# Gate and up of both SwiGLUs by seven block products, their result through DRAM, and down as a stage of its own

## The chip, the cores and the metric

One Trainium2 chip, one of its cores. The metric is the device time of one launch in microseconds, the median of several runs. The engines have the names of the profile: PE (TensorE, with its weight loads as PEld), DVE (VectorE), ACT (ScalarE), POOL (GpSimd), SP (SyncE, which only issues transfers here).

## The reference

One layer of a decoder for 1088 tokens (1024 of a prompt, 8 × 8 of samples), width 1024, inner width 2816. The parts that the change touches are the two SwiGLUs:

```python
def rmsnorm(x, g):
    xf = x.astype(jnp.float32)
    xf = xf * lax.rsqrt(jnp.mean(xf * xf, axis=-1, keepdims=True) + NORM_EPS)
    return (xf * g.astype(jnp.float32)).astype(x.dtype)

def swiglu(x, w_gu, w_down):
    gate, up = jnp.split(x @ w_gu, 2, axis=-1)
    return (jax.nn.silu(gate) * up) @ w_down
...
    h = x + 0.5 * swiglu(rmsnorm(x, lp['norm_ffn1']), lp['ffn1_gu'], lp['ffn1_down'])
    n = rmsnorm(h, lp['norm_mix'])
    proj = n @ lp['w_in']
...
    h = h + jnp.concatenate([o_g, o_s], axis=-1) @ lp['w_out']
    h = h + 0.5 * swiglu(rmsnorm(h, lp['norm_ffn2']), lp['ffn2_gu'], lp['ffn2_down'])
    h = h + jax.nn.sigmoid(rmsnorm(h, lp['norm_ple']) @ lp['ple_gate']) * (p @ lp['ple_proj'])
```

Between `proj` and `h + ...` lies the mixing phase: a gated delta rule and a windowed attention. The last line before the output is the per-layer embedding, followed by a final norm.

## The kernel before

Rows (features) lie on the 128 partitions in eight blocks `k` (KD = 8), tokens on the columns. The 1088 tokens are cut into three column chunks `CH` of 416, 416 and 256. Every fp32 factor of a product is split exactly into two parts (`split`: ScalarE copies the high part, VectorE subtracts to get the low one), and each product is three matmuls: high by high, high by low, low by high (`acc3`). All matmuls are issued from line 172, all splits are lines 198 (ScalarE) and 199 (VectorE).

Inner width 2816 is 22 blocks `f` of 128. For each f, `gu(f)` loads a gate unit and an up unit (512 KB each, tile `raw`), splits them, and computes for each chunk `pg` and `pu`, 24 matmuls each (8 k × 3): 144 per f. The rows that they multiply are `xh`, `xl`, the parts of h·g; the factor 1/rms (`rB`) is multiplied in afterwards, in `finish`, on `pg` and `pu`. So at f = 0 products can begin before 1/rms is known (`nm.split` first, `nm.sums` behind the products). `finish` leaves the result of f in SBUF (`ah`, `al`, three buffers).

After each pair of f, `down` multiplies the pair by its two units of the down weights: 8 row blocks × 3 chunks × 6 matmuls = 144, and VectorE adds each result, halved, to the rows `h` in SBUF (line 362). The rows h stay in SBUF from the input to the mixing norm.

`last` of the first SwiGLU is `mix_norm` (norm of the mixing phase: split and sums, chunk after chunk; rows are saved to DRAM, `scrH`), of the second `embed` (per-layer embedding and final norm). The sums go: squares (ScalarE, added by GpSimd and VectorE), `pss` (TensorE, sums over partitions), ten small VectorE steps for 1/sqrt (`nrt`, `nry`), a diagonal matrix `dg` (VectorE and GpSimd), `pb` (TensorE, broadcast). After the first SwiGLU come 48 small `pm` matmuls for the decay logits, then the projection by `w_in`. At the end of the mixing phase `out_row` and `out_proj` read back the saved rows and add the output projection (tile `pf`), row block after row block.

All loads of weights and inputs are issued by SP, in one order; results to DRAM by ACT. A tile of a pool with n buffers is loaded or written again only when the instructions that read its n-th last content are done.

## Time and profile before

| what | value |
|---|---|
| time, runs shown | 2394.14, 2399.76, 2397.82 us |
| median | 2397.82 us |
| the profiled execution, its span | 2390.8 us (no other time of this execution is given) |
| median less span | 7.0 us |
| TensorE, VectorE, ScalarE, GpSimd busy | 2328.3, 1275.0, 655.0, 255.8 us |
| granted TensorE clock, mean | 0.984 |
| first SwiGLU, mixing phase, second SwiGLU, embedding | about 0 to 810, 810 to 1443, 1443 to 2237, 2237 to 2391 us |

The span goes from the first to the last instruction; the time of a run has some microseconds around it. Busy times of engines overlap, so they do not add up to the span.

### The profile page before, as it was taken

How to read it: one execution, taken by the hardware profiler on the slowest of the kernel's cores; microseconds unless marked ns; L12 is line 12 of the kernel's file. 1: busy time of each engine (PE TensorE's matmuls, PEld its weight loads, DVE VectorE, ACT ScalarE, POOL GpSimd, SP SyncE). 2: the span in 40 equal slices, each digit the busy share in tenths (PEclk: the TensorE clock that was granted, in tenths of full speed). 3: DMA queues.
4: the chain of work that ended last, by engine and by line, in shares of the span. 5: the costliest groups of instructions: out<-in, count | busy, mean ns of one | idle time of the engine just before them, and what ended most of it. 6: DMA issues, size and time to landing. Idle time of an engine off the chain costs nothing.

```text
span 2390.8 us, 34804 instructions
## 1 busy us (share of the span) xinstructions
PE 2328.3 (97%) x14216; PEld 2262.3 (95%) x14216; DVE 1275.0 (53%) x2582; ACT 655.0 (27%) x1345; POOL 255.8 (11%) x242
## 2 busy tenths in 40 slices
PE   7999999999999999989999999999999999999996
PEld 7999999999999898979987899999999999999896
DVE  8544444444444767875654546444444444444847
ACT  6112111112111455321345534111111111211523
POOL 2000000000000234242320120000000000000324
PEclk9999999999999999999997999999999999999998
DMA  4111111111111235455543622111111111111113
GB/s 165 41 49 48 41 50 39 43 47 50 39 51 30 95 113 157 121 148 185 168 155 118 187 70 73 51 36 54 39 51 41 49 36 54 41 49 40 51 44 119
DMA packets 121549, 181.51 MB, mean 76 GB/s; under 512 B 28623, under 2 KB 86735, under 8 KB 121391
## 3 DMA queue, kind: packets, MB, share of 16 engines
q1 hardware_dynamic: 82640, 145.99, 19.2%
q10 hardware_dynamic: 38751, 33.32, 4.5%
q8 instruction: 111, 1.82, 0.3%
q14 instruction: 47, 0.39, 0.1%
HBM read 140.71 MB, written 37.87 MB: 75 GB/s over the span
## 4 chain that ended last, share of the span: by engine, by line
PE 84%; DVE 8%; DMA 3%; ACT 3%; issue 2%; POOL 0%; ACTq 0%; SPq 0%; DVEq 0%; POOLq 0%
PE pg L172 25%; PE pu L172 21%; PE pd L172 21%; PE pm L172 5%; PE pf L172 3%; DVE cv L512 1%; PE pr L172 1%; PE po L172 1%; DVE solve L653 1%; DVE xl L249 1%; PE plv L172 1%; PE pq L172 1%; DVE solve L654 1%; PE px L951 1%; ACT xh L248 1%
## 5 line engine op out<-in xcount | busy, mean ns | idle before, releaser
L172 PE MATMUL pg<-xh,thi 128*128 128x416 f32 (+1 forms) x1248 | 411.4, 330 | 9.0 <-ACT xh L248 6.0
L172 PE MATMUL pg<-xh,tlo 128*128 128x416 f32 (+1 forms) x1248 | 412.2, 330 | 1.3 <-DVE tlo L199 1.3
L172 PE MATMUL pg<-xl,thi 128*128 128x416 f32 (+1 forms) x1248 | 410.5, 329 | 0.6 <-DVE xl L249 0.6
L362 DVE SCALAR_TENSOR_TENSOR h<-pd,h 128x416 f32<-128x416 f32 (+1 forms) x528 | 279.9, 534 | 187.4 <-PE pd L172 184.9
L172 PE MATMUL pd<-ah,dhi 128*128 128x416 f32 (+1 forms) x1056 | 347.5, 329 | 1.8 <-DVE h L362 1.7
L172 PE MATMUL pu<-xh,ulo 128*128 128x416 f32 (+1 forms) x1056 | 347.4, 329 | 1.0 <-DVE ulo L199 1.0
L172 PE MATMUL pu<-xh,uhi 128*128 128x416 f32 (+1 forms) x1056 | 347.4, 329 | 0.7 <-ACT uhi L198 0.7
L172 PE MATMUL pd<-ah,dlo 128*128 128x416 f32 (+1 forms) x1056 | 346.8, 328 | 0.0
L172 PE MATMUL pd<-al,dhi 128*128 128x416 f32 (+1 forms) x1056 | 346.8, 328 | 0.0
L172 PE MATMUL pu<-xl,uhi 128*128 128x416 f32 (+1 forms) x1056 | 344.7, 326 | 0.0
L338 DVE TENSOR_TENSOR tu<-pu,rB 128x416 f32<-128x416 f32 x132 | 70.7, 536 | 352.2 <-PE pu L172 352.2
L172 PEld LDWEIGHTS pg<-xh,thi 128*128 128x128 f32 x1248 | 236.8, 190 | 11.3 <-ACT xh L248 6.3
L172 PEld LDWEIGHTS pg<-xl,thi 128*128 128x128 f32 x1248 | 236.7, 190 | 3.3 <-DVE xl L249 1.0
L172 PEld LDWEIGHTS pg<-xh,tlo 128*128 128x128 f32 x1248 | 236.7, 190 | 2.9 <-DVE tlo L199 1.5
L172 PEld LDWEIGHTS pd<-ah,dhi 128*128 128x128 f32 x1056 | 199.5, 189 | 5.0 <-DVE h L362 3.3
L172 PEld LDWEIGHTS pd<-al,dhi 128*128 128x128 f32 x1056 | 199.6, 189 | 1.5
L172 PEld LDWEIGHTS pd<-ah,dlo 128*128 128x128 f32 x1056 | 199.6, 189 | 1.4
L172 PEld LDWEIGHTS pu<-xh,ulo 128*128 128x128 f32 x1056 | 198.0, 187 | 3.0 <-DVE ulo L199 1.3
L172 PEld LDWEIGHTS pu<-xh,uhi 128*128 128x128 f32 x1056 | 198.8, 188 | 1.6 <-ACT uhi L198 1.1
L172 PEld LDWEIGHTS pu<-xl,uhi 128*128 128x128 f32 x1056 | 198.9, 188 | 1.3
L172 PE MATMUL pm<-xh,thi 128*128 128x416 f32 (+1 forms) x528 | 179.2, 339 | 11.2 <-DVE pre L498 6.4
L172 PE MATMUL pm<-xl,thi 128*128 128x416 f32 (+1 forms) x528 | 178.8, 339 | 0.0
(302 smaller groups left out, 3338.1 us busy)
## 6 DMA issues: line engine op xcount, KB each, us to landing
raw<-in_gu SPq DMA_DIRECT2D x88, 512.0 KB
raw<-in_dn SPq DMA_DIRECT2D x44, 512.0 KB
raw<-in_w_in SPq DMA_DIRECT2D x22, 512.0 KB
raw<-in_gate SPq DMA_DIRECT2D x16, 512.0 KB
raw<-in_w_out SPq DMA_DIRECT2D x14, 512.0 KB
scrT<-cv ACTq DMA_DIRECT2D x8, 544.0 KB
scrK<-tok ACTq DMA_DIRECT2D x8, 512.0 KB
kv<-scrK SPq DMA_DIRECT2D x8, 512.0 KB
```

The source lines that it names most:

```text
L172: i = T.matmul(out, lhsT=lhsT, rhs=rhs, start=start, stop=stop)
L248: S.activation(out=self.h[ci][k], in_=src, func=AF.Copy, scale=g)
L249: V.scalar_tensor_tensor(out=self.l[ci][k], in0=src, scalar=g, in1=self.h[ci][k].bitcast(F32), op0=ALU.mult, op1=ALU.subtract)
L338: V.tensor_tensor(out=tu, in0=pu, in1=nm.r[ci], op=ALU.mult)
L362: V.scalar_tensor_tensor(out=h[m][:, s], in0=pd, scalar=0.5, in1=h[m][:, s], op0=ALU.mult, op1=ALU.add)
L512: V.scalar_tensor_tensor(out=dst, in0=src, scalar=wj, in1=dst, op0=ALU.mult, op1=ALU.add)
L653: V.tensor_tensor(out=tmp[:, :i, :i], in0=X0[:, :i, :i], in1=bc(F[:, :i, i], 1, i), op=ALU.mult)
L654: V.tensor_reduce(out=X0[:, :i, i], in_=tmp[:, :i, :i], axis=AX.X, op=ALU.add, negate=True)
L951: T.transpose(px[:, kv, kb], sc[:, q, kv, kb * P : (kb + 1) * P], ident)
```

## The change

Both SwiGLUs are cut in two parts. `gate_up` takes the tokens in two halves of 544 (`c`), each of two quarters of 272 (QW). For each f and half, gate and up (two row blocks) of two input halves by two token quarters form a 2 × 2 product of blocks, which is computed by seven block products (`WOPS` by `OPS`, 4 k × 3 = 12 matmuls of 272 columns each) instead of eight. `weights(f)` forms and splits the seven weight operands: A11, A12, A22 are the units' halves, S1 to S4 sums that GpSimd makes in place. `operands(c)` loads the rows of a half (`hq`, in the pool `wh`), makes 1/rms, multiplies the rows by g and 1/rms, and forms and splits the seven row operands: B11, B21, B22, and T1 to T4. `hidden` sums the seven products into gate and up, applies Silu and writes the result to DRAM (`scrU`). f = 0 is done for half 0, then the operands of half 1 are made, then f = 0 for half 1; from f = 1 on both halves alternate.

`ffn` then runs down as a stage of its own: rows h are loaded (x, or `scrO` in the second SwiGLU), and for each chunk of CH all 22 f are summed in eight PSUM banks `pd`; the results are read back from `scrU` (`ar`) and split, and the down weights are loaded and split once per chunk, so three times. The norms that follow split and square chunk after chunk, and make the sums of all three chunks after the last. The output projection (`out_half`) works on halves of 544 and leaves its rows in DRAM (`scrO`). `wr` has four buffers instead of two.

```diff
+QW = NT // 4
+HW = NT // 2
+KH = KD // 2
...
-    wr = ctx.enter_context(tc.tile_pool(name="wr", bufs=2))
-    wh = ctx.enter_context(tc.tile_pool(name="wh", bufs=2))
+    wr = pool(ctx, "wr", 4)
+    wh = pool(ctx, "wh", 2)
+    hs = pool(ctx, "hs", 3)
...
+    def unit(src, eng=V):
+        raw = raw_unit(src)
+        w = wh.tile([P, 2, 1024], F32R, tag="t", name="t")
+        split(w[:, 0], w[:, 1], raw, eng)
+        return w[:, 0], w[:, 1]
...
-    def ffn(w_gu, w_dn, gcol, tag, last, first=None):
...
+    scrU = dr.tile([NF, P, NT], F32, name="scrU")
+    OPS = ("B11", "B21", "T2", "T3", "T4", "T1", "B22")
+    WOPS = ("A11", "A12", "S2", "S3", "A22", "S1", "S4")
+    def gate_up(w_gu, gcol, tag, src):
+            xp = [pool(st, tag + "x0", 1, "right"), None]
+            wp = pool(st, tag + "w", 1, "right")
+            tp = pool(st, tag + "t", 2, "right")
+            ps = pool(st, tag + "ps", 8, space=PSUM)
+            xp[1] = pool(st, tag + "x1", 1)
+            X = []
+            def operands(c):
+                def tile_(o, q):
+                    return xp[c].tile([P, KH, QW], F32R, tag=q + o, name=q + o)
+                x = {o: (tile_(o, "h"), tile_(o, "l")) for o in OPS}
+                q = []
+                for i in range(2):
+                    t0 = (2 * c + i) * QW
+                    hq = wh.tile([P, KD, QW], F32, tag="t", name="hq")
+                    for k, n in ((0, 2), (2, 2), (4, 4)) if not X else ((0, 4), (4, 4)):
+                        nc.sync.dma_start(out=hq[:, k : k + n], in_=src[:, k : k + n, t0 : t0 + QW])
+                    acc = tp.tile([P, CW], F32, tag="sum", name="sum", bufs=1)[:, :QW]
+                    squares(tp, [hq[:, k] for k in range(KD)], acc, QW)
+                    r = rms(ps, "m", tp, QW, acc)
+                    for k in range(KD):
+                        V.scalar_tensor_tensor(out=hq[:, k], in0=hq[:, k], scalar=vecs[:, gcol + k : gcol + k + 1], in1=r,
+                                               op0=ALU.mult, op1=ALU.mult)
+                    q.append(hq)
+                    for o, j in (("B11", 0), ("B21", 1)) if i == 0 else (("B22", 1),):
+                        split(*x[o], hq[:, j * KH : (j + 1) * KH])
+                b11, b21, b12, b22 = (q[i][:, j * KH : (j + 1) * KH] for i in range(2) for j in range(2))
+                for o, out, p_, m_, eng in (("T1", b11, b12, b11, V), ("T3", b12, b22, b12, G), ("T2", b22, b22, b11, V), ("T4", b21, b21, b22, V)):
+                    eng.tensor_tensor(out=out, in0=p_, in1=m_, op=ALU.subtract)
+                    split(*x[o], out)
+                return x
+            def weights(f):
+                g, u = (raw_unit(w_gu[f + NF * i]) for i in range(2))
+                (a11, a12), (a21, a22) = ((x[:, :512], x[:, 512:]) for x in (g, u))
+                w = {o: tuple(wp.tile([P, 512], F32R, tag=q + o, name=q + o) for q in ("h", "l")) for o in WOPS}
+                split(*w["A11"], a11)
+                split(*w["A12"], a12)
+                split(*w["A22"], a22)
+                G.tensor_tensor(out=a22, in0=a22, in1=a21, op=ALU.add)
+                G.tensor_tensor(out=a21, in0=a11, in1=a21, op=ALU.subtract)
+                G.tensor_tensor(out=a11, in0=a22, in1=a11, op=ALU.subtract)
+                split(*w["S2"], a11)
+                split(*w["S3"], a21)
+                split(*w["S1"], a22)
+                G.tensor_tensor(out=a12, in0=a12, in1=a11, op=ALU.subtract)
+                split(*w["S4"], a12)
+                return w
+            def hidden(f, w, cs2):
+                I = {}
+                for c in cs2:
+                    I[c] = {n: tp.tile([P, QW], F32, tag=n, name=n) for n in ("p1", "u2", "u3", "s0", "s1")}
+                    I[c]["act"] = hs.tile([P, HW], F32, tag="row", name="act")
+                    I[c]["o0"], I[c]["o1"] = I[c]["act"][:, :QW], I[c]["act"][:, QW:]
+                def product(i, *then):
+                    for c in cs2:
+                        pt_ = ps.tile([P, 512], F32, tag="m", name="p" + WOPS[i])[:, :QW]
+                        (wh_, wl), (xh, xl) = w[WOPS[i]], X[c][OPS[i]]
+                        acc3(pt_, [(wh_[:, j * P : (j + 1) * P], wl[:, j * P : (j + 1) * P], xh[:, j], xl[:, j]) for j in range(KH)])
+                        for out, x in then:
+                            if x is None:
+                                S.copy(I[c][out], pt_)
+                            else:
+                                V.tensor_tensor(out=I[c][out], in0=I[c][x], in1=pt_, op=ALU.add)
+                product(0, ("p1", None))
+                product(1, ("s0", "p1"))
+                for c in cs2:
+                    S.activation(out=I[c]["s0"], in_=I[c]["s0"], func=AF.Silu)
+                product(2, ("u2", "p1"))
+                product(3, ("u3", "u2"))
+                product(4, ("o0", "u3"))
+                for c in cs2:
+                    G.tensor_tensor(out=I[c]["o0"], in0=I[c]["s0"], in1=I[c]["o0"], op=ALU.mult)
+                product(5, ("u3", "u3"), ("u2", "u2"))
+                product(6, ("s1", "u2"))
+                for c in cs2:
+                    S.activation(out=I[c]["s1"], in_=I[c]["s1"], func=AF.Silu)
+                    V.tensor_tensor(out=I[c]["o1"], in0=I[c]["s1"], in1=I[c]["u3"], op=ALU.mult)
+                    nc.scalar.dma_start(out=scrU[f, :, c * HW : (c + 1) * HW], in_=I[c]["act"])
+            w0 = weights(0)
+            X.append(operands(0))
+            hidden(0, w0, (0,))
+            X.append(operands(1))
+            hidden(0, w0, (1,))
+            for f in range(1, NF):
+                hidden(f, weights(f), (0, 1))
+    def ffn(w_gu, w_dn, gcol, tag, src, last):
+        gate_up(w_gu, gcol, tag, src)
+        st = ExitStack()
+        xg = pool(st, tag + "xg", 1)
+        fr = ExitStack()
+        h1 = pool(fr, tag + "h", 1, "right").tile([P, KD, NT], F32, name="h")
+        fp = pool(fr, tag + "f", 2, "right")
+        ps = pool(fr, tag + "pd", 8, space=PSUM)
+        h = [h1[:, k] for k in range(KD)]
+        for ci, (c0, w) in enumerate(CH):
+            nc.sync.dma_start(out=h1[:, :, c0 : c0 + w], in_=src[:, :, c0 : c0 + w])
+        end = last(xg, ps, fp, h1, h)
+        next(end)
+        for ci, (c0, w) in enumerate(CH):
+            pd = [ps.tile([P, 512], F32, tag="m", name="pd")[:, :w] for m in range(KD)]
+            for f in range(NF):
+                wf = blocks(unit(w_dn[f]))
+                a = fp.tile([P, CW], F32, tag="ar", name="ar", bufs=3)[:, :w]
+                nc.sync.dma_start(out=a, in_=scrU[f, :, c0 : c0 + w])
+                ah, al = (fp.tile([P, CW], F32R, tag=t, name=t)[:, :w] for t in ("ah", "al"))
+                split(ah, al, a)
+                for m in range(KD):
+                    mm(pd[m], wf[m][0], ah, start=f == 0, stop=False)
+                    mm(pd[m], wf[m][0], al, start=False, stop=False)
+                    mm(pd[m], wf[m][1], ah, start=False, stop=f == NF - 1)
+            for m in range(KD):
+                V.scalar_tensor_tensor(out=h[m][:, c0 : c0 + w], in0=pd[m], scalar=0.5, in1=h[m][:, c0 : c0 + w], op0=ALU.mult, op1=ALU.add)
+            next(end)
+        next(end, None)
+        fr.close()
+        return st, xg
...
+    def mix_norm(xg, ps, fp, h1, h):
+        nm = Norm(xg, h, ps, "m", fp, G_MIX)
...
         for ci, (c0, w) in enumerate(CH):
             nm.split(ci)
+            nc.scalar.dma_start(out=scrH[:, :, c0 : c0 + w], in_=h1[:, :, c0 : c0 + w])
+            nm.squares(ci)
+            yield
+        for ci in range(len(CH)):
             nm.sums(ci)
...
+    def out_half(m, w, late):
         w = blocks(w)
+        row = hs.tile([P, HW], F32, tag="row", name="row")
+        c0 = HW * late
+        nc.sync.dma_start(out=row, in_=scrH[:, m, c0 : c0 + HW])
+        for i in range(2):
+            po = pps.tile([P, 512], F32, tag="m", name="pf")[:, :QW]
+            s = slice(c0 + i * QW, c0 + (i + 1) * QW)
             fill[0] = True
+            acc3(po, [w[k] + tuple(x[:, s] for x in oh[k]) for k in range(KD)])
             fill[0] = False
+            dst = row[:, i * QW : (i + 1) * QW]
             V.tensor_tensor(out=dst, in0=dst, in1=po, op=ALU.add)
+        nc.scalar.dma_start(out=scrO[:, m, c0 : c0 + HW], in_=row)
```

Not shown: the fixed order of the mixing phase is changed in a few places, `embed` loads its operands into tiles of its own, and a parameter of the build sets the size of a DMA scratch area.

The first place is VectorE at the start of the first SwiGLU. Before, behind the split of the first gate unit, its queue has the low parts of h·g of chunk 0 (`h_78` are the rows), which the first products read:

```order
L199 TENSOR_TENSOR tlo_156<-raw_153,thi_155 128x1024
L249 SCALAR_TENSOR_TENSOR xl0_0_126<-h_78,vecs_68,xh0_0_102 128x416
L249 SCALAR_TENSOR_TENSOR xl0_1_127<-h_78,vecs_68,xh0_1_103 128x416
L249 SCALAR_TENSOR_TENSOR xl0_2_128<-h_78,vecs_68,xh0_2_104 128x416
L249 SCALAR_TENSOR_TENSOR xl0_3_129<-h_78,vecs_68,xh0_3_105 128x416
L268 TENSOR_TENSOR acc_241<-acc_241,sq1_253 128x416
```

After, there stand behind the second rsqrt of half 0 (`dg_276` is its diagonal; `hq_154` and `hq_225` are the two quarters, `pb_275` the broadcast 1/rms) the row multiplies and then the eight wide passes that form and split operands:

```order
L301 TENSOR_TENSOR dg_276<-ident_69,np_272 128x16
L337 SCALAR_TENSOR_TENSOR hq_225<-hq_225,vecs_71,pb_275 128x272 x8
L381 TENSOR_TENSOR s0_309<-p1_306,pA12_326 128x272
L344 TENSOR_TENSOR hq_154<-hq_225,hq_154 128x1088
L203 TENSOR_TENSOR lB22_153<-hq_225,hB22_152 128x1088
L203 TENSOR_TENSOR lT1_151<-hq_154,hT1_150 128x1088
L344 TENSOR_TENSOR hq_225<-hq_225,hq_154 128x1088
L203 TENSOR_TENSOR lT3_147<-hq_225,hT3_146 128x1088
L344 TENSOR_TENSOR hq_154<-hq_154,hq_225 128x1088
L203 TENSOR_TENSOR lT2_145<-hq_225,hT2_144 128x1088
L203 TENSOR_TENSOR lT4_149<-hq_154,hT4_148 128x1088
```

What moved: the row operands now come behind 1/rms, and four of them behind a chain of sums. On SP the rows of half 1 are asked for behind the weights of f = 1 and 2; `hq_430` takes the buffer that `hq_225` leaves after the split of T2, `hq_500` that of `hq_154` after the split of T4:

```order
L207 DMA raw_690<-in_gu1 128x1024
L207 DMA raw_692<-in_gu1 128x1024
L207 DMA raw_946<-in_gu1 128x1024
L207 DMA raw_948<-in_gu1 128x1024
L332 DMA hq_430<-in_x 128x4x272 x2
L332 DMA hq_500<-in_x 128x4x272 x2
```

The second place is SP between gate and up and down of the first SwiGLU. Before, no such place exists: loads of gate and up units (`in_gu1`) and of down units (`in_dn1`) alternate to the end:

```order
L204 DMA raw_5967<-in_gu1 128x1024
L204 DMA raw_5973<-in_gu1 128x1024
L204 DMA raw_6155<-in_dn1 128x1024
L204 DMA raw_6161<-in_dn1 128x1024
L204 DMA raw_6359<-in_gu1 128x1024
L204 DMA raw_6365<-in_gu1 128x1024
L204 DMA raw_6547<-in_dn1 128x1024
L204 DMA raw_6553<-in_dn1 128x1024
```

After, six down units, then the rows of h in three transfers (4.46 MB), which wait for the memory that the products of half 0 leave at f = 21, then the first results:

```order
L207 DMA raw_6219<-in_dn1 128x1024
L207 DMA raw_6254<-in_dn1 128x1024
L207 DMA raw_6289<-in_dn1 128x1024
L417 DMA h_6077<-in_x 128x8x416 x2
L417 DMA h_6077<-in_x 128x8x256
L425 DMA ar_6119<-scrU_75 128x416
L425 DMA ar_6154<-scrU_75 128x416
```

What moved: the rows h are loaded there, ahead of the first result row `ar_6119`, by the same engine.

The third place is TensorE behind the last down product of the first SwiGLU. Before (`pd` down, `pm` logits):

```order
L172 MATMUL pd_6743<-ah_5979,dlo_6550 128x256
L172 MATMUL pd_6743<-ah_6371,dhi_6555 128x256
L172 MATMUL pd_6743<-al_6372,dhi_6555 128x256
L172 MATMUL pd_6743<-ah_6371,dlo_6556 128x256
L172 MATMUL pm_7077<-xh0_0_6751,w2_7074 16x416
L172 MATMUL pm_7077<-xl0_0_6775,w2_7074 8x416
```

After (`pss`, `pb` of the three chunks' norms, `rB0` to `rB2` their sums of squares):

```order
L176 MATMUL pd_7763<-al_8507,t_8501 128x256
L176 MATMUL pd_7763<-ah_8506,t_8501 128x256
L176 MATMUL pss_8581<-ones_70,rB0_6103 128x2 x3
L176 MATMUL pss_8581<-ones_70,rB0_6103 32x2
L176 MATMUL pb_8605<-dg_8606,ones_70 128x416
L176 MATMUL pss_8615<-ones_70,rB1_6104 128x2 x3
L176 MATMUL pss_8615<-ones_70,rB1_6104 32x2
L176 MATMUL pb_8605<-dg_8610,ones_70 128x416
L176 MATMUL pb_8639<-dg_8640,ones_70 128x416
L176 MATMUL pss_8649<-ones_70,rB2_6105 128x2 x2
L176 MATMUL pb_8639<-dg_8644,ones_70 128x416
L176 MATMUL pb_8669<-dg_8670,ones_70 128x256
L176 MATMUL pb_8669<-dg_8673,ones_70 128x256
L176 MATMUL pm_8735<-xh0_6087,w2_8732 16x416
L176 MATMUL pm_8735<-xl0_6095,w2_8732 8x416
```

What moved: the three pairs of sums and broadcasts stand ahead of the logits.

## Rows read from the trace of the kernel before

**Rows 1.** The page's first part: busy us, share, instructions.
```profile
span 2390.8 us, 34804 instructions
PE 2328.3 (97%) x14216; PEld 2262.3 (95%) x14216; DVE 1275.0 (53%) x2582; ACT 655.0 (27%) x1345; POOL 255.8 (11%) x242
```

**Rows 2.** Busy time of each engine in two stretches, granted clock, DMA share, GB/s.
```profile
60.00:120.00 60.00, 60.00 (x372) 59.58 (x371) 31.42 (x53) 11.87 (x18) 0.00 (x0) 1.00 0.13 44
1500.00:1560.00 60.00, 60.00 (x357) 59.54 (x356) 26.73 (x46) 8.10 (x12) 0.00 (x0) 1.00 0.11 36
```

**Rows 3.** Chain that ended last, first SwiGLU: start, us, engine, tile, line, count.
```profile
67.74 4.55 PE pg L172 x24
72.28 4.53 PE pu L172 x24
...
85.89 2.86 PE pg L172 x24
88.74 2.88 PE pu L172 x24
91.62 23.91 PE pd L172 x144
```

**Rows 4.** The same chain at the second SwiGLU's start.
```profile
1443.46 4.55 PE pg L172 x24
...
1517.20 12.84 PE pd L172 x68
```

**Rows 5.** Groups by line and shape: busy us, mean ns, idle before.
```profile
L199 DVE TENSOR_TENSOR tlo<-raw,thi 128x1024 fp32r<-128x1024 f32 x74 | 90.6, 1224 | 31.5 <-ACT thi L198 30.8 <-issue 0.3
L362 DVE SCALAR_TENSOR_TENSOR h<-pd,h 128x416 f32<-128x416 f32 x352 | 205.9, 589 | 143.7 <-PE pd L172 143.7
L362 DVE SCALAR_TENSOR_TENSOR h<-pd,h 128x256 f32<-128x256 f32 x176 | 74.1, 423 | 43.7 <-PE pd L172 41.3
L249 DVE SCALAR_TENSOR_TENSOR xl<-h,vecs,xh 128x256 fp32r<-128x256 f32 x32 | 15.5, 514 | 0.0
L299 DVE TENSOR_TENSOR dg<-ident,np 128x32 fp32r<-128x32 f32 x10 | 8.2, 816 | 0.0
L192 DVE TENSOR_TENSOR nrt<-nrt,nv 128x4 f32<-128x4 f32 x30 | 6.2, 207 | 0.7
L871 DVE TENSOR_TENSOR xq<-xq,rot 128x1088 f32<-128x1088 f32 x4 | 5.2, 1289 | 3.6 <-POOL rot L869 3.6
L198 ACT CAST thi<-raw 128x1024 fp32r<-128x1024 f32 x96 | 100.8, 1050 | 122.4 <-PE pg L172 56.8 <-PE pm L172 34.7 <-PE pf L172 14.5
L621 POOL TENSOR_TENSOR gu<-ctile,gp 128x512 fp32r<-128x512 f32 x16 | 19.8, 1262 | 0.7 <-PE pdc L172 0.6
L268 POOL TENSOR_TENSOR rB<-rB,sq 128x256 f32<-128x256 f32 x12 | 10.6, 882 | 13.3 <-ACT sq L267 13.3
L869 POOL TENSOR_TENSOR rot<-rot,rope 128x1088 f32<-128x1088 f32 x5 | 18.3, 3655 | 15.5 <-DMA rot<-xq 10.5 <-DMA rot<-xk 5.0
```

**Rows 6.** A transfer in the chain at the start, and one stretch's busy times.
```profile
2.59 7.21 DMA h<-in_x
10.00:14.00 4.00, 4.00 (x17) 3.53 (x15) 4.00 (x6) 4.00 (x9) 1.61 (x2) 1.00 1.04 399
```

**Rows 7.** Chain, then TensorE's timeline, at the ends of both SwiGLUs' down.
```profile
784.34 12.47 PE pd L172 x66
810.15 0.28 PE L172 MATMUL pd<-ah,dlo 128*128 128x256 f32 x1
824.02 0.55 PE L172 MATMUL pm<-xh,thi 128*128 128x416 f32 x1
824.37 0.55 PE L172 MATMUL pm<-xl,thi 128*128 128x416 f32 x1
2238.55 0.43 PE L172 MATMUL pg<-xh,thi 128*128 128x416 f32 x1 [1.00 <-DVE h L362]
```

More of the change, by code (lines that the diff above doesn't have):

```diff
@@ L250, in split, with squares @@
                                        op0=ALU.mult, op1=ALU.subtract)
+        def squares(self, ci):
+            c0, w = CH[ci]
+            squares(self.tp, [x[:, c0 : c0 + w] for x in self.rows], self.r[ci], w)
         def sums(self, ci):
-            squares(self.tp, ci, self.r[ci])
-            S.copy(self.r[ci], rms(self.ps, self.tag, self.tp, ci, self.r[ci]))
-    def squares(tp, ci, acc):
-        c0, w = CH[ci]
+            S.copy(self.r[ci], rms(self.ps, self.tag, self.tp, CH[ci][1], self.r[ci]))
+    def squares(tp, rows, acc, w):
         half = (acc, tp.tile([P, CW], F32, tag="acc", name="acc", bufs=1)[:, :w])
@@ L261, in squares, with rms @@
             for k in range(q, KD, 2):
-                src = h[k][:, c0 : c0 + w]
                 if k == q:
-                    S.activation(out=half[q], in_=src, func=AF.Square)
+                    S.activation(out=half[q], in_=rows[k], func=AF.Square)
                 else:
                     sq = tp.tile([P, CW], F32, tag=f"sq{q}", name=f"sq{q}")[:, :w]
-                    S.activation(out=sq, in_=src, func=AF.Square)
+                    S.activation(out=sq, in_=rows[k], func=AF.Square)
                     eng.tensor_tensor(out=half[q], in0=half[q], in1=sq, op=ALU.add)
         V.tensor_tensor(out=acc, in0=acc, in1=half[1], op=ALU.add)
-    def rms(ps, tag, tp, ci, acc):
-        c0, w = CH[ci]
+    def rms(ps, tag, tp, w, acc):
         nt = (w + P - 1) // P
@@ L287, in rms @@
                                     scalar1=1.0 / D, scalar2=EPS, op0=ALU.mult, op1=ALU.add)
-            r = rsqrt(xg, v, [P, nt], "nr")
-            parts = xg.tile([P, 2, NTT], F32R, tag="np", name="np", bufs=2)[:, :, :nt]
+            r = rsqrt(cst, v, [P, nt], "nr")
+            parts = cst.tile([P, 2, NTT], F32R, tag="np", name="np", bufs=2)[:, :, :nt]
             V.tensor_copy(parts[:, 0], r)
@@ L409, in decoder_layer @@
     pw = pt = pool(ppst, "ppt", OPT["t"], space=PSUM)
-    right.close()
-    rows = pool(ctx, "rows", 1, "right")
     right = ExitStack()
@@ L1038, in mix_split @@
     def mix_split(k, late):
-        c0, c1 = (CH[1][0], NT) if late else (0, CH[1][0])
+        c0, c1 = (HW, NT) if late else (0, HW)
         gt = pp.tile([P, NT], F32, tag="pre", name="gt")[:, c0:c1]
@@ L1157, in decoder_layer @@
             w = ws.pop(0)
-        out_proj(m, w, range(1, len(CH)))
+        out_half(m, w, True)
         next_weight()
@@ L1219, in final_r @@
             c0, w = CH[ci]
-            r = rms(pn, "m", fp, ci, fa[:, c0 : c0 + w])
+            r = rms(ps, "m", fp, w, fa[:, c0 : c0 + w])
             S.copy(nm.r[ci], r)
```

167 lines of the change are left out of this document (41 added, 126 removed).

## The prediction

> **What bounds the kernel now.** I read the page first: of a span of 2390.8 us TensorE is busy in 97%, VectorE in 53% [rows 1]. Then the busy times by stretch, because the mean hides the stages: inside both SwiGLUs TensorE has 60.00 of 60 us, VectorE 27 to 31, ScalarE 8 to 12, GpSimd nothing, at a granted clock of 1.00 (the 2.4 GHz level) and a DMA share of 0.11 to 0.13 [rows 2]. So a SwiGLU costs what its matmuls cost. Then the chain that ended last, for the price of one: 24 matmuls of 416 columns take 4.53 us, 188.8 ns each, 24 of 256 columns 2.87 us, 119.4 ns [rows 3]. The price is not proportional to columns: the line through both points is 8.4 ns + 0.434 ns per column. One f (gate and up, 144 matmuls) takes 4 × 4.535 + 2.86 + 2.88 = 23.88 us, the down of two f 23.91 [rows 3].
>
> **Gate and up, f = 1 to 21.** After: 7 products × 12 matmuls × 2 halves = 168 matmuls of 272 columns. The trace has none of this width; 272 lies between two widths that it has, near 256, so the line holds it well: 126.4 ns (at least 119.4, at most 188.8 × 272/416 + a few = 128). 168 × 126.4 = 21.24 us, 2.64 less per f; 42 such f: **−111 us**. This needs the rest of f hidden under 21.24. Per f, from the groups in [rows 5]: VectorE 7 splits of 512 (about 0.65, half of 1.22), 14 sums and 2 products of 272 (0.44): 11.6 us; ScalarE 7 casts (0.55), 2 copies, 4 Silu: 6.5; GpSimd 4 × 1.26 + 2 × 0.9 = 6.8. One stretch is serial: A22 of f+1 can be cast only when f's A22 products end (at 15.2 of 21.24), then GpSimd's four sums run one after another (5.05), and S2's low part is needed at 6.07 of f+1. Cast, split and waits end about 22.5, 27.3 is needed: 5 us of cover, hidden.
>
> The Trainium skill ("TensorE: Matmul & The Clock Gate", Back-to-back issue gap) gives columns/2.4 + 2.5 ns for a gap at the full clock. By that 272 columns would take 115.8 ns as an estimate, and the sum below would come 75 us lower; the rows differ from it (at 416 it would say 175.8 where they show 188.8), and they decide.
>
> **The start of a SwiGLU.** Before, f = 0 ran on rows h·g while 1/rms was still being made; counted back from the first down (91.62 − 2 × 23.88), f = 1 began at 43.9 us. After, the operands need 1/rms first, as the second rows of the order show. I walk it with the durations of [rows 5]. First half: 2.2 MB had landed at 9.8 us [rows 6], and after the change the first quarter is complete at the same count of bytes; the second quarter (1.11 MB at 399 GB/s) at 12.6. GpSimd's adds of the squares stand between its weight sums: 4 × 1.26 + 6 × 0.9 from about 8 puts the second quarter's sum at 18.7, and VectorE's queue holds that sum ahead of the end of the first rsqrt. Then 5 small steps of 0.2, the diagonal (0.42 + 0.82): 21.5; 8 row multiplies (about 0.55): 27; B11, B21 split, second chain: 33; 8 multiplies: 37.6; T1 1.29, T3 on GpSimd 3.66: 43; five more VectorE passes of 1.29: last split at 49.5. Second half: its load waits for a buffer that the split of T2 frees (48.2), so nothing of it overlaps: landed 53.3, sums 57 and 60.4, chains and multiplies 78.5 (two weight splits stand between), T1 80.8, T3 84.5, five passes: 91. Then 26 matmuls (3.3), and 4.5 for TensorE at its lower level after the idle time and for passes next to GpSimd: f = 1 at 98.8, **+55 us** (45 to 65). Second SwiGLU: before 1517.20 − 47.76 − 1443.46 = 26.0 us after the mixing's last product [rows 4]. After, its first load waits for the last two output products, for a buffer: second quarter landed 5 us after the end E, 7.6 earlier than in the walk, weight sums already done (−4): f = 1 at E + 87, **+61 us** (50 to 70).
>
> **Down as its own stage.** Its matmuls are the same in number and width: no change. Hidden per f of 256 columns (2.87 us): 0.66 MB, 228 GB/s, under the 399 that the queue reached; VectorE 1.22 + 0.42, ScalarE 1.05 + 0.41. Its start is not hidden: the three loads of h (4.46 MB) wait for S4's product of the first half of f = 21, that is 1.5 us before the last, and the first result row stands behind them on the same queue. 4.46 MB / 399 = 11.2, some 2 to start, 0.5 for the row, 1.1 for cast and split, minus 1.5: TensorE is idle some 13 to 15 us and then 3 us slower at 1.2 GHz (a step of 0.35 between matmuls of 416 columns instead of 0.189 [rows 7]): **+18 us** each (4 if the row doesn't queue, 22 at a slower load). The Trainium skill ("DMA: Bandwidth & Descriptors", Queues, rings and completion order) says that SP's queue is consumed in ring order on each engine, by which the row would wait for all of h; no row here shows it for these transfers. From chunk to chunk 8 evacuations (0.42 to 0.59) must free the eight banks, with splits between: 2.5 each, twice, **+5** per SwiGLU (0 to 8).
>
> **The ends.** Before, a SwiGLU's last pd is at 810.15, the first projection matmul at 824.02, 13.9 later, and in these lie 8 us of the logits' matmuls [rows 7]. After, the sums of all three chunks come behind the last pd and ahead of the logits: VectorE has 3 evacuations, 8 low parts, 4 adds (some 6.5 us), and three chains of 10 × 0.2 + 0.4 + 1.2: 17 to 19 us without TensorE, then 8 of logits, and the lower level: **+15** (10 to 20). At the second end the same 19.5 + 3 stand where 1.0 stood [rows 7] and two shorter waits (about 4.5): **+17** (12 to 22). The output projection: 96 × 126.4 = 12.13 us per row block instead of 24 × (2 × 188.8 + 119.4) = 11.93: **+2**. What falls away: before, the last down of each SwiGLU ended late for the norm's work beside it (784.34 + 23.91 = 808.25, seen 810.4; about 3.6 in the second): **−6**.
>
> **Sum:** 55 + 61 − 111 + 2 × 18 + 2 × 5 + 15 + 17 + 2 − 6 = **+79 us**. Made against the profiled span, 2390.8 → 2470; the median of the runs lies 7.0 above the span (2397.8), so 2477. Measurements tell 0.2% (5 us) from no change.
>
> **Rivals.**
> 1. Faster: the 272-column pace. 42 × 168 = 7056 matmuls, so 1 ns is 7.06 us. Without the overhead, at 272/2.4 = 113.3 ns, the sum is −13: 2384. It decides at 126.4 − 79/7.06 = 115.2 ns; from there on down it is faster. For it: only two widths were measured. Against: both carry 13 to 16 ns over columns/2.4 [rows 3]. 5%, and 4% for a pace at which nothing changes. By the rule of the Trainium skill named above (Back-to-back issue gap), 115.8 ns, it would end at 2402.
> 2. Gate and up not bound by TensorE: GpSimd's serial sums next to VectorE's passes eat the 5 us of cover. At 1.5 us per f: +63, 2540. For it: the fourteen weight tiles have a single buffer each. Against: the cover is a quarter of f. 11%.
> 3. The result rows do not queue behind h: 4 instead of 18 twice, 2449. For it: other queues and 16 engines share the load. Against: same issuing engine. 16%.
> 4. Down's third chunk (256 columns) too short for its loads and splits: 3.4 instead of 2.87 us for 22 f, twice: +23, 2500. 11%.
> 5. That it doesn't do what it says: no; 168 for 144 matmuls of two thirds of the columns is read from the order.
>
> **How the numbers follow.** The forecast holds 50%: 2477. Its terms' bounds (±10 for each start, −14 to +4 for each down, ±5 for each end, −5 to +3 for each chunk row) give 2445 to 2505 when not all fall together. The range reaches to rivals 3, 4 and half of 2: 2432 to 2520. Faster 8% (rival 1, and 3 for what I didn't see), the same 4%, slower 88% (the forecast and rivals 2 to 4).
>
> **What would show it.** f = 2 to 20 in 21.2 us each with TensorE full; the first f = 1 block near 99 us; some 15 us of idle TensorE at each start of down, released by the DMA of ar; 17 to 20 us at each end, released by VectorE. Wrong would be: an f of 20 us or less (rival 1), idle TensorE inside f with S2 or S3 as releaser (2), down's idle time near 4 us (3), pd blocks of 24 matmuls of 256 columns over 3 us (4), or starts under 70 us, which the shared buffer would have to allow.

## The result, and the profile after

After the change the kernel took 2511.43 us (median of 4 runs, 2508.67 to 2520.85), the kernel before measured beside it 2395.98: ratio 1.0476, 95% interval 1.0422 to 1.053. The forecast was 2477, its range 2432 to 2520. The profiled execution has a span of 2510.3 us against 2390.8 [rows 1], 119.5 longer; it is laid out stage by stage below.

The page's first part, as in [rows 1]: TensorE's work fell by 85 us (2328.3 to 2243.0), yet its share fell from 97% to 89%, so some 200 us of idle time are new.
```profile
span 2510.3 us, 40123 instructions
PE 2243.0 (89%) x15476; PEld 2184.7 (87%) x15476; DVE 1475.8 (59%) x2822; ACT 860.8 (34%) x1765; POOL 616.0 (25%) x518
```
Busy times by stretch, as in [rows 2]: the start of the first SwiGLU, gate and up, and the gap ahead of down.
```profile
60.00:120.00 60.00, 31.80 (x213) 30.70 (x212) 47.21 (x96) 19.49 (x35) 16.88 (x16) 0.72 0.11 36
150.00:300.00 150.00, 150.00 (x1199) 150.00 (x1199) 97.22 (x165) 44.89 (x92) 57.15 (x44) 1.00 0.23 77
...
552.00:566.00 14.00, 0.00 (x0) 0.00 (x0) 0.00 (x0) 0.46 (x1) 0.00 (x0) 0.51 1.04 375
```
Inside gate and up nothing but TensorE limits: 150.00 of 150 us at granted clock 1.00, VectorE at 65%. Where TensorE ran full from 60 to 120 us before, it now has 31.80 of 60, at a mean granted clock of 0.72. And ahead of down there are 14 us in which the engines compute nothing but 0.46 us on ScalarE, while the DMA moves 375 GB/s.

The chain of waits in gate and up, answering to [rows 3]:
```profile
1604.14 3.00 PE pA L176 x24
1607.14 6.01 PE pS L176 x48
```
48 matmuls of 272 columns in 6.01 us are 125.2 ns each. One f takes 21.0 us instead of 23.88; the 21 f from 107.07 to 549.87 take 442.8, 21.09 each with the waits of the first ones.

TensorE's timeline, with the idle time before a row and its releaser in brackets. First the start (f = 1 begins with the row of 107.07), then down in the first SwiGLU with its end, then the second SwiGLU's down and end.
```profile
16.88 1.16 PE L176 MATMUL pss<-ones,sum 128*128 128x2 f32 x6 [16.88 <-DVE sum L272]
24.15 0.60 PE L176 MATMUL pb<-dg,ones 128*128 128x272 f32 x1 [6.12 <-DVE dg L301]
34.42 0.59 PE L176 MATMUL pb<-dg,ones 128*128 128x272 f32 x1 [8.35 <-DVE dg L301]
51.34 0.82 PE L176 MATMUL pS<-hT,hS 128*128 128x272 f32 x2 [10.80 <-ACT hT L202]
63.22 0.74 PE L176 MATMUL pss<-ones,sum 128*128 128x2 f32 x6 [1.42 <-DVE sum L272]
70.12 0.60 PE L176 MATMUL pb<-dg,ones 128*128 128x272 f32 x1 [6.16 <-DVE dg L301]
80.39 0.59 PE L176 MATMUL pb<-dg,ones 128*128 128x272 f32 x1 [8.35 <-DVE dg L301]
97.66 0.82 PE L176 MATMUL pS<-hT,hS 128*128 128x272 f32 x2 [11.87 <-ACT hT L202]
...
107.07 0.28 PE L176 MATMUL pA<-hB,hA 128*128 128x272 f32 x1
...
566.13 3.14 PE L176 MATMUL pd<-ah,t 128*128 128x416 f32 x8 [16.26 <-ACT ah L202]
680.28 0.45 PE L176 MATMUL pd<-al,t 128*128 128x416 f32 x1 [2.70 <-DVE al L203]
775.81 0.39 PE L176 MATMUL pd<-al,t 128*128 128x256 f32 x1 [2.69 <-DVE al L203]
781.92 0.58 PE L176 MATMUL pd<-al,t 128*128 128x256 f32 x1 [3.00 <-DVE al L203]
...
840.36 0.28 PE L176 MATMUL pd<-ah,t 128*128 128x256 f32 x1
...
852.65 0.72 PE L176 MATMUL pb<-dg,ones 128*128 128x416 f32 x1 [11.29 <-DVE dg L301]
...
873.17 0.46 PE L176 MATMUL pm<-xh,t 128*128 128x416 f32 x1
...
1494.76 0.29 PE L176 MATMUL pf<-oxh,t 128*128 128x272 f32 x1
...
1591.27 0.28 PE L176 MATMUL pA<-hB,hA 128*128 128x272 f32 x1
...
2051.74 0.71 PE L176 MATMUL pd<-ah,t 128*128 128x416 f32 x1 [17.66 <-ACT ah L202]
...
2329.94 0.28 PE L176 MATMUL pd<-ah,t 128*128 128x256 f32 x1
...
2343.00 0.72 PE L176 MATMUL pb<-dg,ones 128*128 128x416 f32 x1 [12.07 <-DVE dg L301]
```
The operands of a half need two chains (the first from pss to pb in 7 us) in a row, and the second half repeats all of it from 63.22 on. The broadcast of a quarter's 1/rms is two pb matmuls, for the high and the low part of its diagonal. Those of the second quarter don't stand together: the first starts at 34.42, the second behind 18 matmuls of the first two products, and VectorE waits for it. A row of TensorE's timeline and one of VectorE's:
```profile
38.89 0.43 PE L176 MATMUL pb<-dg,ones 128*128 128x272 f32 x1
39.36 3.35 DVE L337 SCALAR_TENSOR_TENSOR hq<-hq,vecs,pb 128x272 f32<-128x272 f32 x8 [4.99 <-PE pb L176]
```
SyncE's timeline says what down waits for:
```profile
548.41 5.45 SPq L417 DMA_DIRECT2D h<-in_x  x3
553.91 5.50 SPq L425 DMA_DIRECT2D ar<-scrU  x3
```
The rows of the result are issued behind three loads of h (4.46 MB) on one queue, and TensorE starts at 566.13. Two rows of VectorE's timeline say what the wait of 680.28 in chunk 1 is for:
```profile
671.63 2.89 DVE L251 SCALAR_TENSOR_TENSOR xl<-h,vecs,xh 128x416 fp32r<-128x416 f32 x2
679.65 0.58 DVE L203 TENSOR_TENSOR al<-ar,ah 128x416 fp32r<-128x416 f32 x1
```
From 664.88 on VectorE empties the eight banks of chunk 0 and makes the low parts (xl) and squares' sums of the norm that follows; the low part of chunk 1's third row comes only at 679.65.

### The profile page after: what moved, and what is told of

Same layout as the page of the kernel before. It is cut to its first block, busy times and chain, and to the rows that moved or that the text cites. A ratio compares the mean times of both kernels' runs of the same rounds, so it can differ in the third digit from the quotient of the medians.

```text
span 2510.3 us, 40123 instructions
## 1 busy us (share of the span) xinstructions
PE 2243.0 (89%) x15476; PEld 2184.7 (87%) x15476; DVE 1475.8 (59%) x2822; ACT 860.8 (34%) x1765; POOL 616.0 (25%) x518
## 5 line engine op out<-in xcount | busy, mean ns | idle before, releaser
L176 PE MATMUL pd<-ah,t 128*128 128x416 f32 (+1 forms) x2112 | 512.6, 331 | 36.1 <-ACT ah L202 35.4
L176 PEld LDWEIGHTS pd<-ah,t 128*128 128x128 f32 x2112 | 379.2, 192 | 38.5 <-ACT ah L202 36.7
L176 PE MATMUL pd<-al,t 128*128 128x416 f32 (+1 forms) x1056 | 336.8, 331 | 17.1 <-DVE al L203 17.1
L176 PE MATMUL pS<-hT,hS 128*128 128x272 f32 x1056 | 307.2, 292 | 45.5 <-ACT hT L202 45.5
L176 PE MATMUL pS<-hT,lS 128*128 128x272 f32 x1056 | 306.9, 291 | 0.8 <-DVE lS L203 0.8
L176 PE MATMUL pS<-lT,hS 128*128 128x272 f32 x1056 | 306.6, 291 | 0.0
L176 PE MATMUL pm<-xh,t 128*128 128x416 f32 (+1 forms) x1056 | 270.8, 338 | 13.1 <-DVE pre L561 7.9
L176 PE MATMUL pA<-lB,hA 128*128 128x272 f32 x704 | 206.0, 293 | 0.0
L176 PE MATMUL pA<-hB,hA 128*128 128x272 f32 x704 | 205.8, 292 | 0.0
L176 PE MATMUL pA<-hB,lA 128*128 128x272 f32 x704 | 205.7, 292 | 0.0
```

The source lines that it names most:

```text
L176: i = T.matmul(out, lhsT=lhsT, rhs=rhs, start=start, stop=stop)
```

## The experiments

**Theory:** gate and up gain what the rows say (TensorE-bound at 125.2 ns), and the loss lies in serial places at the seams: operands before the first product, the first result rows behind h, the norm chains at the ends. **Rival:** a seam that is shortened hands its wait to the next, or the loss lies within the stages. Medians of the kernel before, measured beside the runs below: 2394.01 (e1 to e4), 2392.1 (e5 to e7), 2395.83 (e8, e9), 2392.18 (e10).

**e1: the loads of h behind the third result row**
```
-        for ci, (c0, w) in enumerate(CH):
-            nc.sync.dma_start(out=h1[:, :, c0 : c0 + w], in_=src[:, :, c0 : c0 + w])
-        end = last(xg, ps, fp, h1, h)
-        next(end)
...
                 split(ah, al, a)
+                if ci == 0 and f == 2:
+                    for k0, v in CH:
+                        nc.sync.dma_start(out=h1[:, :, k0 : k0 + v], in_=src[:, :, k0 : k0 + v])
+                    end = last(xg, ps, fp, h1, h)
+                    next(end)
```


> Down's first three result rows are asked for ahead of the rows h (and of what the next stage loads), nothing else is changed. Theory A (at the start of down TensorE waits for a row that stands behind 4.46 MB on the same queue): the idle 16.3 and 17.7 us fall to 1 to 4 each, and the following 3 us at 1.2 GHz with them; the time falls by 28 to 38 us, to about 2478. Theory B (the round trip through DRAM itself, or the last results landing, sets the start): idle stays over 10 us each, the time falls by less than 10. Theory C (the rows only move the wait to the fourth row, which now stands behind h): idle at the start is near 0, but TensorE waits 8 to 12 us at the fourth row; the time falls by 5 to 12.

Measured: 2514.96 us, 1.0505 (1.0458 to 1.0551). TensorE's timeline at the first down:
```profile
550.91 1.43 PE L176 MATMUL pd<-ah,t 128*128 128x416 f32 x6 [1.48 <-ACT ah L202]
568.49 2.98 PE L176 MATMUL pd<-ah,t 128*128 128x416 f32 x8 [3.69 <-ACT ah L202]
```
16.26 became 1.48, and 3.69 came back at the fourth row, which now stands behind h: the first pb of the end came at 841.68 instead of 852.65. So queuing behind h is shown for the first SwiGLU. In the second the order still had h first, and 16.37 us of idle time stayed. The medians don't tell this kernel from the changed one. In the profiled executions (2505.2 against 2510.3) the 11 us won by the first pb are lost again: the mixing stage, whose instructions the edit doesn't touch, took 11 us longer (more on it at the end).

**e2: the loads of h on ScalarE's queue**
```
-            nc.sync.dma_start(out=h1[:, :, c0 : c0 + w], in_=src[:, :, c0 : c0 + w])
+            nc.scalar.dma_start(out=h1[:, :, c0 : c0 + w], in_=src[:, :, c0 : c0 + w])
```


> The rows h are loaded by ScalarE's queue instead of SP's, order of the program unchanged. Theory A (order within one queue): the first result row lands early, TensorE idle 2 to 6 us at each start of down instead of 16.3 and 17.7; the time falls by 24 to 34 us. Theory B (the sixteen engines are full for 12 us with h whichever queue it comes from, and a row issued with it gets its share only slowly): idle 8 to 14, the time falls by 5 to 15.

Measured: 2505.08 us, 1.0463 (1.0423 to 1.0504); idle 8.25 and 9.53 instead of 16.26 and 17.66. ScalarE's timeline:
```profile
550.14 2.08 ACTq L417 DMA_DIRECT2D h<-in_x  x1
552.34 4.82 ACTq L397 DMA_DIRECT2D scrU<-act  x2
557.20 0.98 ACT L202 CAST ah<-ar 128x416 fp32r<-128x416 f32 x2 [6.66 <-issue]
```
The wait was halved and moved: ScalarE, which must cast the first row, stood 4.82 us in the issue of its own stores behind h. The idle time is in theory B's range, but its cause (full DMA engines) is not what the rows show: the first result rows had been issued at 533.28, and ahead of h the DMA engines stood idle:
```profile
544.00:549.00 5.00, 5.00 (x42) 5.00 (x41) 2.01 (x6) 0.16 (x1) 0.77 (x1) 1.00 0.00 0
```
So the row was there, and the engine that casts it was not. The total is not told apart from the changed kernel's; in the profiled execution the mixing stage took 638.0 us instead of 621.6.

**e3: one chain for both quarters of a half**
```
                     squares(tp, [hq[:, k] for k in range(KD)], acc, QW)
-                    r = rms(ps, "m", tp, QW, acc)
...
+                for i, r in enumerate(rms_n(ps, "m", tp, [(QW, s) for s in accs])):
+                    hq = q[i]
```


> In the operands of a half, one sum over partitions, one rsqrt chain and one pair of diagonals per half instead of one per quarter. Theory A (the start of a SwiGLU is a serial chain on VectorE, and the second quarter's chain stands behind the first one's multiplies: the 8.35 us of idle TensorE ahead of its broadcast): each of the four halves gets 5 to 8 us shorter, the time falls by 20 to 30 us, to about 2486. Theory B (VectorE's passes and GpSimd's subtraction are what fills the start, the chain lies in their shadow): the time falls by less than 8 us.

Measured: 2500.8 us, 1.0467 (1.0428 to 1.0506), span 2496.6. The last pS wait of the first start came at 85.69 instead of 97.66, in the second SwiGLU 11.7 earlier too: the starts gave 23.7. The edit does two things at once: it saves a chain per half, and it puts all four pb matmuls of a half ahead of the first product, so VectorE's sixteen multiplies run without the wait of 4.99 us seen above:
```profile
27.64 6.61 DVE L379 SCALAR_TENSOR_TENSOR hq<-hq,vecs,pb 128x272 f32<-128x272 f32 x16
```
So theory A's gain arrived, but no run separates the chain from the order on TensorE. The ratio of the total is not told apart from the changed kernel's 1.0476. Chunk 1 of down, counted from its wait to that of chunk 2 (680.28 to 775.81 in the changed kernel), took 99.1 us instead of 95.5, with the same matmuls; e4 had the same (98.8), e1 and e2 had not (95.5, 97.1).

**e4: one chain for the three chunks at each end**
```
-        for ci in range(len(CH)):
-            nm.sums(ci)
+        nm.all_sums()
```


> At the end of each down the sums of all three chunks go through one rsqrt chain instead of three one after another; the per-half chains stay as they are. Theory A (the ends are three serial chains): TensorE's idle time there, 11.3 + 3.2 + 2.5 and 12.1 + 3.2 + 2.5 us, loses 4 to 6 each; the time falls by 8 to 12 us, to about 2501. Theory B (the wait is the last chunk's low parts and squares on VectorE, chains ride along): the first broadcast comes as much later as the others come sooner; the time falls by less than 4.

Measured: 2511.74 us, 1.0496 (1.047 to 1.0522). The ends became 3.8 us (29.05 instead of 32.82 from the last pd to the projection) and 5.5 us shorter (174.9 instead of 180.4 from the last pd to the span's end); the total shows nothing of it, and down had the slower pace of e3.

**e5: 64 unused bytes in the first pool.** In e3 and e4 the first pool had grown, and everything above it lay 64 bytes from where it was.
```
     vecs = cst.tile([P, NVEC], F32, name="vecs")
+    gap = cst.tile([P, 16], F32, name="gap")
```


> One unused tile of 64 bytes is put into the first pool, so that every later buffer of the changed kernel lies 64 bytes higher (the down weights' tile t at a multiple of 128 instead of 64 over one); no instruction of the path changes. In the two runs that changed the chains, the down stage's matmuls of 416 columns were spaced 0.191 us instead of 0.187. Theory (the place of the operands in SBUF sets that pace): spacing 0.191, chunk 1 of down 99 us instead of 95.5, the kernel 8 to 12 us longer, 2519 to 2523. Rival (the pace came from the other edits, from the order or the DMA beside it): spacing 0.187, 2511 within 5.

Measured: 2525.26 us, 1.0544 (1.0503 to 1.0585). TensorE's timeline in chunk 1, three consecutive groups of the changed kernel, then three of e5:
```profile
692.17 1.85 PE L176 MATMUL pd<-ah,t 128*128 128x416 f32 x9
696.65 1.84 PE L176 MATMUL pd<-ah,t 128*128 128x416 f32 x9
701.13 1.85 PE L176 MATMUL pd<-ah,t 128*128 128x416 f32 x9
```
```profile
694.49 1.87 PE L178 MATMUL pd<-ah,t 128*128 128x416 f32 x9
699.05 1.89 PE L178 MATMUL pd<-ah,t 128*128 128x416 f32 x9
703.68 1.87 PE L178 MATMUL pd<-ah,t 128*128 128x416 f32 x9
```
24 matmuls take 4.48 us, with the gap 4.56 and 4.63 in turn: 186.8 against 191.5 ns a matmul. The edit changes nothing but places, so the place in SBUF sets that pace, and that of e3 and e4 is explained. The price in the total is not shown: chunks 0 and 1 of the first SwiGLU are 3.5 longer each, but its chunk 2 is 2.2 shorter (a second wait of 1.49 instead of 3.00), down as a whole 4.8 and 0.7 longer, and the mixing stage, which varies by itself, 4.8. My 8 to 12 was too much for what the pace does.

**e6: eight plain products in the same staging**
```
-    OPS = ("B11", "B21", "T2", "T3", "T4", "T1", "B22")
-    WOPS = ("A11", "A12", "S2", "S3", "A22", "S1", "S4")
+    OPS = ("B11", "B21", "B12", "B22")
+    WOPS = ("A11", "A12", "A21", "A22")
...
+                        s = tp.tile([P, QW], F32, tag="s0", name="s0")
+                        S.activation(out=s, in_=pt[0], func=AF.Silu)
+                        V.tensor_tensor(out=act[:, i * QW : (i + 1) * QW], in0=s, in1=pt[1], op=ALU.mult)
```


> Gate and up by the eight plain block products over the same halves of 544 tokens and 272 columns, result via DRAM and down as its own stage as in the changed kernel: 192 matmuls instead of 168 per tile and half, 4 operand pairs instead of 7 per half, no sums of blocks. Theory (gate/up is TensorE-bound at 125.1 ns per matmul, the stages around it cost what they cost whatever the products): 22 x 48 x 0.1251 = 132 us more in each SwiGLU less what the shorter preparation of operands saves at the two starts (two starts of 63 and 70 us over the old ones, of which the sums and splits of three operands and their late matmuls are 10 to 20 each): 2511 + 264 - 20 to 40 = 2735 to 2755; period 24.0 us. Rival (the seven products' sums on VectorE or the DMA pace the tile): period 21 to 23 us, 2620 to 2700.

The expected sum counts the 24 extra matmuls of a tile twice; by its own period of 24.0 it should have read +132 in all, 2603 to 2623. Measured: 2553.57 us, 1.0657 (1.0605 to 1.0709). Two rows of its chain of waits:
```profile
87.94 2.99 PE pg L176 x24
...
112.06 2.99 PE pg L176 x24
```
The period is 24.12 us, so the theory of the pace holds. But f = 1 begins (counted back 21 periods from down's start) at 75.8 and 64.4 after the last output matmul, against 107.07 and 96.4: 31 and 32 us earlier. That is more than the sums T1 to T4 alone: without them, and without the weights' sums, the buffers of the rows come free earlier too, and the second half's first pss starts at 39.15 instead of 63.22. Down's starts wait 5.60 and 8.27. So the seven products earn 127 us in the steady part (2 × 21 × 3.03 of periods 24.12 and 21.09) and pay 63 of it at the starts; the staging itself, with plain products, stands 161 us over the kernel before.

**e7: all seams at once.** Squares summed on TensorE, one chain per half, the second half's rows in buffers of their own, result rows one unit ahead of TensorE and ahead of h, the third chunk's sums two to a bank so that two chunks' chains run under it. Like e8 to e10 it carries the unused tile of e5, which with the larger first pool puts the down weights back at 64 bytes over a multiple of 128; down's step is 187 ns again.
```
+                for k in range(KD if sq else 0):
+                    s = tp.tile([P, QW], F32, tag="sqr", name="sqr", bufs=3)
+                    S.activation(out=s, in_=acc[k], func=AF.Square)
+                    for t in (0, 2, 1):
...
-            pd = [ps.tile([P, 512], F32, tag="m", name="pd")[:, :w] for m in range(KD)]
+            banks = [ps.tile([P, 512], F32, tag="m", name="pd") for m in range(KD // n)]
+            pd = [banks[m // n][:, m % n * w : (m % n + 1) * w] for m in range(KD)]
...
+                if f < NF - 1 or ci < len(CH) - 1:
+                    got = load(ci, f + 1) if f < NF - 1 else load(ci + 1, 0)
```


> The changed kernel with its serial places overlapped: squares summed by TensorE and one chain of rows for both quarters of a half; the second half's rows loaded beside the first's; rows of the result loaded and split one unit ahead, in buffers of their own, ahead of the residual; the third chunk of down with two sums to a bank, so that the first two chunks' norm chains run under it, one chain for both. Theory (the loss of the change is in those serial places: starts +63 and +70, down starts +16 and +18, ends +18 and +27): a half's chain -24 (measured), down starts -30, ends -25 to -40, starts -20 to -40 more: 2511 - 100 to 135 = 2375 to 2410. Rival (each place only hands its wait to the next one, as the moved residual loads did): 2440 to 2480. The span of the mixing stage may move either by 15 with its clock.

Measured: 2463.52 us, 1.0287 (1.0247 to 1.0328): 48 us less than the changed kernel, under half of what was expected and within the rival's range. Down's idle time at its start was 1.48 in both SwiGLUs, the ends 8 and 10 shorter, the starts nearly unchanged (f = 1 at 104.8). Its chain of waits shows why:
```profile
7.46 17.60 PE pss L178 x96
```
The squares' sums took TensorE 17.6 us per half, a new wait made by the edit.

**e8: squares back on GpSimd and VectorE**
```
+                    half = [acc] if c else [acc, tp.tile([P, QW], F32, tag="u3", name="acc")]
...
+                            S.activation(out=sq, in_=q[i][:, k], func=AF.Square)
+                            (G, V)[z].tensor_tensor(out=half[z], in0=half[z], in1=sq, op=ALU.add)
...
+                        split(*x[o], q[i][:, j * KH : (j + 1) * KH], V if o == "B11" else G)
```


> e7 with its miss at the two starts mended: squares again summed by GpSimd and VectorE (in e7 TensorE took 17.6 us per half for them, and the second half's came behind the first half's products), the second half's squares by ScalarE and GpSimd alone so that they run under the first half's work, the low parts of two blocks subtracted on GpSimd, and at the ends the last chunk's squares ahead of its split. Theory (VectorE's own work, 18 us per half, is all that is left at a start): the second tile starts 75 to 85 us after the program's start and 65 to 75 after the last output matmul (104.8 and 95 in e7, 107.1 and 96.4 in the changed kernel), ends 3 shorter each: 2463 - 45 to 65 = 2400 to 2420. Rival (the second half's rows still end behind the first half's products, through memory that is handed on): 2445 to 2460.

Measured: 2451.85 us, 1.0239 (1.0209 to 1.027); f = 1 at 92.1 and, in the second SwiGLU, 82.9 after the last output matmul (e7: 104.8 and 94.3). Better by 13 and 11, not by the 20 to 30 expected. The chain of waits:
```profile
44.94 1.71 POOL sum L388
46.71 1.70 POOL sum L388
...
53.58 0.79 POOL sum L388
54.43 0.78 POOL sum L388
...
59.18 0.77 PE pss L178 x6
```
The second half's squares began only at 41.4, behind the first half's casts on ScalarE, and GpSimd's sums carried the chain.

**e9: gate/up's weights moved by 32 bytes**, to 64 over a multiple of 128 bytes, where down's weights lie in the changed kernel.
```
+            wq = pool(st, tag + "wq", 1, "right").tile([P, 8], F32, name="wq")
             wp = pool(st, tag + "w", 1, "right")
```


> e8 with 32 unused bytes ahead of gate/up's weight blocks, so that they lie 64 over a multiple of 128 bytes (96 in the changed kernel and in e8) as the down weights do in the changed kernel. Theory (the place of the weights in SBUF sets the pace there too, as 64 bytes did in down: 186.8 against 191.5 ns for 416 columns): the 272-column matmul 120 to 124 ns instead of 125.2, the period of a tile 20.2 to 20.8 us instead of 21.04, e8 less 10 to 35 us. Rival (only 0 against 64 matters, or only in down): 125.2 ns, e8 within 5.

Measured: 2455.43 us, 1.0263 (1.023 to 1.0297); 150 us of gate and up hold 1197 matmuls, 1199 in e8. No gain: 64 over 128 is no rule for every stage.

**e10: squares of both halves first, h behind the ninth unit**
```
+            early = [rows(0), rows(1)]
             X.append(operands(0, *early[0]))
...
+                    tc.add_manual_dep(ld.ins, im.ins.name, NOSYNC, reason="behind the first rows of the result")
```


> e8 with the second half's rows loaded and squared before the first half's operands are made (in e8 ScalarE took them up at 41.4 us, behind the first half's casts, and the second chain began at 59.2), and the residual of down held behind the first nine units so that the first result rows have the queue to themselves (3.6 us at the fourth row in e8). Theory (the second half's chain is what separates the halves, VectorE's 18 us per half what is left): the second tile starts 72 to 80 us after the program's start (91.7 in e8) and 65 to 73 after the last output matmul (85.2), the row waits at down's start are gone: 2452 - 30 to 45 = 2407 to 2422, still above the kernel before. Rival (VectorE is in order and the second half's operands wait for the first half's evictions on it, so an earlier chain only waits longer): 2440 to 2455.

Measured: 2444.48 us, 1.0226 (1.017 to 1.0283), not told apart from e8. Its chain of waits:
```profile
54.97 1.14 PE pss L178 x12
...
57.72 0.44 DVE s L440
58.66 0.44 DVE act L455
...
61.07 0.61 PE pb L178
```
The second half's sums are ready, but its pss stands behind the first half's products on TensorE, and its diagonal behind the first half's evictions on VectorE: the multiplies begin at 62.55 instead of 65.10, and f = 1 at 89.8. The first half paid for it too: GpSimd summed the second half's squares beside its chain, and its first pb came at 28.74 instead of 25.56. The rival held for the starts; the row waits of the first down are gone (273.5 us from its first pd to its last, 276.8 in e8). Nothing here beats the kernel before, and no run points to a version that would.

## Why the prediction was right, step by step

By stage, from the rows above and [rows 3, 4, 7], in us of the profiled spans:

| step | forecast | measured | from |
|---|---|---|---|
| gate and up, 42 f | −111 | −117.4 | 2 × 21 × 23.88 before; 107.07 to 549.87 and 1591.27 to 2034.08 after |
| start 1 / 2 | +55 / +61 | +63.2 / +70.4 | 107.07 − 43.9; 1591.3 − 1494.9 − 26.0 |
| down 1 / 2, start and chunks | +23 / +23 | +27.6 / +33.0 | 16.26 + (274.2 − 262.9); 17.66 + (278.2 − 262.9) |
| end 1 / 2 | +15 / +17 | +18.9 / +26.8 | 32.8 − 13.9; 180.4 − 153.5 from last pd to the span's end |
| mixing | +2 | +2.3 | 621.7 − 619.4 |
| before's late downs | −6 | −5.9 | the last down of two f took 25.97 and 27.51 instead of 23.79 |
| sum | +79 | +119 | span +119.5 |

- **Gate and up:** right. 125.2 ns against 126.4 from the line through [rows 3]; e6 shows the same pace with other products, so rival 2 (GpSimd and VectorE behind TensorE) and rival 1 (a pace of 115 ns) are out. The Trainium skill ("TensorE: Matmul & The Clock Gate", Back-to-back issue gap) would have said 115.8 by its formula, which it gives for an isolated matmul; the measurement decides.
- **Starts:** the serial path was right, each term 8 to 9 too small. The largest step that the walk lacked is TensorE's order. It let the second quarter's multiplies follow their diagonal and end at 37.6; the diagonal was ready at 34.4, but the second pb stood behind 18 matmuls of products (34.42 to 38.89), and the multiplies ended at 42.7. The second half repeats that (80.39 to 84.75; walked 78.5, seen 88.4). The first chain of a half was too short as well: the walk took 1/rms as five small steps and a diagonal, some 3 us; from pss to pb it took 7.3 and 6.9 (16.88 to 24.15, 63.22 to 70.12). e3 takes a chain and the wait for pb out of each half at once, and the start is 12 shorter; which part of that is the order alone was not run. e6 adds that half of a start goes with T1 to T4, the weights' sums and the buffers that they hold.
- **Down's start:** idle time 16.26 and 17.66 against 13 to 15; shown by e1 to be the queue. Rival 3 is out. The Trainium skill ("DMA: Bandwidth & Descriptors", Queues, rings and completion order) has a queue's descriptors taken in ring order on each engine; 16.26 against 1.48 agrees.
- **Chunks:** mis-sized, and not by the wait that was meant. TensorE passes from one chunk to the next without waiting for a bank. It waits at the third row of chunk 1 (2.70) and at the second and third of chunk 2 (2.69, 3.00), because VectorE makes their low parts only behind the evacuations and the norm's own low parts: 8.4 together, against 5. The lower clock (granted 0.50) took 1.5 us at the start of down 1, not 3, and 2.5 behind the last wait; the matmuls of 416 columns are 2 ns faster than before, 2 us in all. That makes the 11.3 by which down 1 is longer within 1 us. Down 2 is 4.0 longer still: some 2.5 more at the lower clock, and 1.9 in its row f = 20, where ScalarE's cast came late. The third chunk itself is full (2.8 to 2.9 us per f from f = 4 on): rival 4 is out.
- **Ends:** TensorE's idle time is what was walked: 17.0 and 17.8 us, against 17 to 19. The pss and pb matmuls between the waits (6 us) and 9.4 us of logits instead of 8 are what was put too low at the first end. At the second, the seam itself grew by 22.6, near the 21.5 of the walk; but the embedding behind it, which was to be 4.5 shorter, is 4.2 longer (156.5 against 152.3 us): two waits of 5.35 and 5.39 for broadcasts are new there. What put them there was not run.

All misses of the seams have one sign: they were walked with their longest instructions, without the order on TensorE, the norm's work on VectorE and the small steps between. Together they are +46, less the −6 of the pace. 2511 lies above the 2505 to which the terms' bounds were said to reach; the range held it because it reached on towards rival 2, which did not happen. In that the prediction was lucky.

## What to carry to other kernels

Fewer matmuls pay per unit, the staging they need pays per stage: here 59 us a SwiGLU against seams of 110 and 130 (start, down, end), of which e10 still left 68 and 87. Before rewriting a stage, count every 1/rms chain, every sum of operands and every queue that stands ahead of its first matmul, at the price from its first to its last instruction, and look whether the matmuls of one broadcast stand together. When a seam is shortened, look at once for the engine that is next in order: in e1, e2, e7 and e10 the wait came back on another engine or row.
